# A hybrid diffusion layer on one core: the issue orders of five engine queues replaced in four stretches of the program

## The chip, the core and the metric

The kernel runs on one core of one Trainium2 chip. The metric is the device time of one execution in microseconds (us); the number that counts is the median over runs. The core's engines are named as in the profile: PE multiplies matrices (PEld loads its weights), DVE, ACT and POOL work on tiles in the on-chip memory, and SP does nothing here but issue DMA transfers. Each engine works off its own instruction queue strictly in order and waits at its head for what the next instruction needs.

## The reference, cut to what matters

One layer is applied to 512 latent and 128 context tokens (T = 640 together) of width D = 1024. The latent path in full (the context path is the same with one-dimensional convolutions):

```
mod = silu(cond) @ w_ada + b_ada                  # six vectors: sh1, sc1, g1, sh2, sc2, g2
h = rms_norm(x, g_mix_pre) * (1 + sc1) + sh1
z, xbc, dt_raw, cf_in = split(h @ w_in)
xbc = silu(dwconv1d(xbc, w_ssd_conv))
y = ssd(xbc, dt_f) + flip(ssd(flip(xbc), dt_b)) + xs * d_skip     # scans, forward and backward, 16 heads
y_ssd = rms_norm(y * silu(z), ssd_norm)
u = silu(layer_norm(dwconv1d(cf_a * sigmoid(cf_g), w_cf_conv)))   # 31 taps
x = x + g1 * rms_norm(concat(y_ssd, u) @ w_out, g_mix_post)
h = rms_norm(x, g_ffn_pre) * (1 + sc2) + sh2
f = (silu(gate) * val) @ w_down          # gate, val = halves of dwconv2d(h @ w_up), 3x3
x = x + g2 * rms_norm(f, g_ffn_post)
```

Outputs are both token sets and the two final scan states of the context.

## The kernel before, in words

**Layout.** Tokens lie along the free dimension, channels on the 128 partitions, so x is eight tiles `T_1` to `T_8` of 128x640 f32. Every large product is made in three matmuls of reduced precision: a weight tile `wr` of 128x1024 is split by ACT into a rounded part `wh` (line 320) and by POOL into the remainder `wl` (line 322), an activation into `H` (hi, ACT, line 409) and another `H` (lo, DVE, line 411), and `mm3` (line 424) adds w1·xh, w1·xl and w2·xh, each for 384 and 256 columns. Weight tiles come by SP into two buffers, `wh` and `wl` have three.

**Stages.** (1) First stage: SP loads the conditioning `cts`, the eight x tiles, 32 tiles of the adaLN weight (`in_wada`, 256 KB each, four groups of eight), the constants `csts` (the identity is in it), `prms`, `wdts` and the first projection weights (`wr_186`, `wr_192`, 512 KB each). ACT applies silu to `cts` (line 501), loads the table for the square root with a dummy instruction on `epsc` (line 503), and squares the x tiles into four rotating slots (line 507); PE sums the columns with a vector `ones` that POOL sets (lines 264 and 482); ACT takes the root (line 496), DVE the reciprocal (line 497), and PE spreads the result over the partitions with the identity (line 490). `ada_first(s)` multiplies one group of adaLN tiles with `cts` (line 450), ACT copies the sum to `adar` (line 453), PE transposes it (line 432) and DVE writes `modv` (line 441). DVE multiplies x by the spread reciprocal (line 532) and applies scale and shift (line 543); then hi, lo, the small product for dt (line 516) and the first three projections follow. (2) First quarter: the other projections, the two convolutions and eight pairs of scan heads. For each pair, rows of accumulated decays are loaded again from DRAM (`S<-acD`, lines 687 and 692), ACT subtracts them with a relu per chunk (line 798) and exponentiates (lines 782, 805); `ssd_states` copies states out of PSUM (line 757, tiles `S` or `AT`), POOL chains them, and PE uses them (lines 816, 827). (3) Middle norm: output projection, norm, `ada_half` for the second modulation (lines 465 to 472). (4) FFN up, convolution, down. (5) Tail: for each half of the columns `out_sums` (colsum, root, reciprocal), `out_spread` (line 1442; ACT copies the spread to `HL`, line 1446), `out_apply` (line 1449; multiply 1455, add 1456, store 1457), where POOL does pieces 0, 3 and 6 and DVE the other five.

**What sets the order.** The program text makes all instructions and their dependencies; the table `ORDER` (lines 49 to 172) then gives for each of the engines PE, DVE, Activation, Pool and SP a permutation of its instructions, as ranges of their numbers in program order. `issue_in_order` (line 175) ties each instruction to the one that the table puts ahead of it. So the table alone sets each queue, and the tiles, buffers and arithmetic come from the text. SP issues each DMA in that order as well, and a DMA waits for the one eight places ahead of it, whose semaphore it uses again.

Of the kernel before, what the change touches and what calls it, by code (L numbers as in the profile page):

```python
# [50 lines left out]
0-31 36-49 32-34 50-53 35 54-90 104-105 102-103 91-101 116-119 106 120-126 107-115 127 187-191 175-180 192  # L51
181-182 193 173-174 140-172 194-196 183-186 211-242 197-198 258-259 243 128-129 246-252 260-263 130-139
199-210 270 253-257 264-265 284-289 244-245 282-283 320-327 271-281 290-291 266-269 296 292-294 308-311
297-298 295 312-319 299-307 328-332 341-374 399-402 375-378 403 379-385 404 386-388 405-434 447-450 435-445
451-464 446 465-487 495 488-492 496-506 493-494 507-522 543-550 523 551-560 524-535 561-567 536 568-574
537-542 575-590 645-648 333-335 649-684 336-339 685-690 693-719 691-692 720-725 340 389-393 726-758 789-796
759 394-398 797-799 760-768 595 591-594 800-803 769-776 804-818 777-788 819-836 878-916 596-603 608 604-607
926-931 917-923 932-946 924-925 947-970 974-983 971-973 984-1005 609-620 1006-1014 1022 621-644 1023-1028
1015-1019 1029 1020-1021 1030-1048 837-841 1070-1073 1049 1074-1087 1050-1056 1088-1094 1057-1069 1095-1117
846-849 842-845 854-857 850-853 1118-1146 1207-1213 1147 1214-1216 1148-1163 1217 1164-1165 874-877 858-873  # L60
1218-1226 1255-1256 1227-1249 1257-1275 1250-1251 1276-1283 1252-1254 1284-1290 1170 1166-1169 1291-1294
1303-1314 1295-1302 1315-1337 1351-1352 1338-1350 1353-1374 1450-1452 1375-1381 1453-1470 1382-1398
1171-1178 1183-1186 1179-1182 1471-1484 1187-1206 1485-1517 1546 1518 1547-1554 1519-1521 1399-1403
1522-1524 1555-1556 1525 1557-1567 1526-1532 1568-1577 1533-1545 1578-1609 1683-1684 1610-1623 1404-1408
1624-1626 1685-1700 1627-1641 1701-1718 1409-1432 1441-1442 1433-1435 1443-1444 1436-1440 1719-1723
1731-1743 1724-1729 1744-1745 1730 1746-1755 1449 1445-1448 1756-1811 1827-1830 1812-1814 1642-1646
1815-1823 1831-1835 1824-1826 1836-1866 1916 1867 1917-1918 1647-1682 1919 1868-1869 1920 1870-1874
1921-2010 2012-2017 2011 2018-2022 1875-1879 2023-2080 2149-2150 2081-2089 2151-2157 2090-2103 2158-2164
2104-2107 2165-2179 1884-1887 1880-1883 1892-1895 1888-1891 2197-2201 1912-1915 1896-1911 2202-2244
2180-2196 2357-2386 2112 2108-2111 2245-2272 2387-2416 2117-2120 2113-2116 2417-2446 2125-2128 2121-2124  # L70
2145-2148 2129-2144 2447-2467 2507-2518 2468 2519 2273-2276 2317-2320 2277-2280 2321-2324 2469-2476
2520-2531 2477-2491 2325-2335 2341-2344 2336-2340 2281-2290 2492-2495 2291-2300 2496-2506 2532 2301-2310
2533-2534 2311-2312 2345-2352 2535-2545 2313-2316 2546-2552 2567-2585 2553-2562 2586-2593 2563-2566 2594
2353-2356 2597-2613 2595-2596 2614-2615 2810-2829 2759-2770 2645-2648 2621-2637 2649 2638-2639 2650-2658
2640-2641 2659-2661 2642-2644 2693-2704 2616-2620 2669-2676 2705-2709 2662-2668 2717 2710-2711 2677-2682
# [12 lines left out]
3397-3398 3374-3375 3380-3387 3399 3410-3412 3406-3409 3376-3377 3391 3378 3392-3393 3400-3402 3413-3414
# [1517 lines left out]
```

## Time and profile before

| | |
|---|---|
| runs | 976.6, 978.75 and 983.1 us, median 978.75 us |
| the profiled execution: own time, span | 980.17 us, 978.4 us |
| busy, share of the span | PE 945.8 us (97%), PEld 922.5 (94%), DVE 685.0 (70%), POOL 580.2 (59%), ACT 472.3 (48%) |
| the last chain, by engine | PE 89%, DMA 4%, ACT 2%, DVE 2% |
| DMA | 117.52 MB, mean 120 GB/s over the span |

The span runs from the first to the last instruction of the profiled execution; the execution's own time is 1.8 us longer. Idle time of PE is what is left to gain as long as the work stays the same, so the views used below list for an engine when it stood still and which instruction released it. In the lists of a timeline each row is a start, a duration, an engine, a line and an operation; in brackets stands the idle time just before and its releaser. The view of windows gives busy time per engine (with the number of instructions), the clock granted to PE, the share of time in which the DMA engines moved data, and the rate.

### The profile page before, as it was taken

The numbers are of one execution on the slowest core, as the hardware profiler recorded it, in microseconds if no ns is written. First come the engines' busy times: TensorE is split into PE (matmuls) and PEld (weight loads), VectorE is DVE, ScalarE is ACT, GpSimd is POOL, SyncE is SP. The second block draws the span as 40 slices with busy tenths as digits, with TensorE's granted clock in tenths as the row PEclk, the third lists the DMA queues.
The fourth block names the chain that finished last, engine by engine and source line by source line (L and its number), as shares of the span: only waits on it lengthen the run. The fifth ranks groups of instructions, "written<-read, shape, count | busy, mean of one in ns | idle before, by whom it ended". The sixth has DMA issues, their size and how long they took to land.

```text
span 978.4 us, 18784 instructions
## 1 busy us (share of the span) xinstructions
PE 945.8 (97%) x7623; PEld 922.5 (94%) x7623; DVE 685.0 (70%) x1076; ACT 472.3 (48%) x799; POOL 580.2 (59%) x416
## 2 busy tenths in 40 slices
PE   4999999999999999999999999999999999999995
PEld 2899999899999998999989999999999999999995
DVE  1769898888989997633576897998988898400004
ACT  4345665877568495822454843323233336322211
POOL 1334699798999882634761997444454436543434
PEclk9999999999999999999999999999999999999998
DMA  9622424434325342589661243222222231322213
GB/s 344 254 71 83 121 82 127 117 100 146 118 84 161 87 125 76 160 274 325 204 213 56 68 168 97 80 83 69 87 65 86 66 87 55 96 67 76 82 38 108
DMA packets 50294, 117.52 MB, mean 120 GB/s; under 512 B 6016, under 2 KB 13952, under 8 KB 50208
## 3 DMA queue, kind: packets, MB, share of 16 engines
q1 hardware_dynamic: 50208, 116.33, 37.4%
q8 instruction: 60, 0.98, 0.4%
q14 instruction: 26, 0.21, 0.1%
HBM read 112.55 MB, written 3.75 MB: 119 GB/s over the span
## 4 chain that ended last, share of the span: by engine, by line
PE 89%; DMA 4%; ACT 2%; DVE 2%; issue 1%; POOL 1%; SPq 1%; POOLq 0%; ACTq 0%
PE ps L424 75%; PE ps L1268 2%; PE pq L424 2%; PE pq L827 2%; PE pq L469 2%; PE pq L816 1%; DMA T<-in_wada 1%; DMA S<-acD 1%; PE pq L753 1%; PE pq L450 1%; DMA S<-in_wada 1%; DMA wr<-in_wup 1%; PE pq L1268 1%; PE pq L601 1%; PE pq L490 1%
## 5 line engine op out<-in xcount | busy, mean ns | idle before, releaser
L322 POOL TENSOR_TENSOR wl<-wr,wh 128x1024 fp32r<-128x1024 f32 (+3 forms) x127 | 290.5, 2291 | 320.3 <-ACT wh L320 297.7
L424 PE MATMUL ps<-H,wh 128*128 128x384 f32 (+1 forms) x1636 | 316.9, 309 | 0.1
L424 PE MATMUL ps<-T,wh 128*128 128x384 f32 (+1 forms) x1472 | 272.7, 306 | 0.3 <-ACT S L1236 0.3
L320 ACT ACTIVATE wh<-wr 128x1024 fp32r<-128x1024 f32 (+3 forms) x131 | 131.3, 1003 | 288.8 <-PE ps L424 179.9
L1246 DVE SCALAR_TENSOR_TENSOR S<-ps,prms,S 128x441 f32<-128x441 f32 (+2 forms) x336 | 233.4, 695 | 28.9 <-ACT S L1236 18.3
L424 PEld LDWEIGHTS ps<-H,wh 128*128 128x128 f32 x1636 | 249.8, 188 | 2.9 <-issue 1.7
L424 PEld LDWEIGHTS ps<-T,wh 128*128 128x128 f32 x1472 | 218.9, 188 | 0.8 <-ACT S L1236 0.6
L881 DVE SCALAR_TENSOR_TENSOR ps<-u,prms,ps 128x655 f32<-128x655 f32 x205 | 185.1, 903 | 12.0 <-ACT ps L878 6.1
L424 PE MATMUL ps<-H,wl 128*128 128x384 f32 (+1 forms) x818 | 191.6, 309 | 0.0
L424 PE MATMUL ps<-T,wl 128*128 128x384 f32 (+1 forms) x736 | 166.2, 305 | 0.0
L424 PEld LDWEIGHTS ps<-H,wl 128*128 128x128 f32 x818 | 129.1, 188 | 1.0 <-issue 1.0
L497 DVE RECIPROCAL rsm<-rsm 128x160 f32<-128x160 f32 (+2 forms) x9 | 7.4, 817 | 152.0 <-ACT rsm L496 152.0
L424 PEld LDWEIGHTS ps<-T,wl 128*128 128x128 f32 x736 | 113.0, 188 | 0.0
L424 PE MATMUL ps<-S,wh 128*128 128x384 f32 (+1 forms) x420 | 88.1, 310 | 0.0
L424 PEld LDWEIGHTS ps<-S,wh 128*128 128x128 f32 x420 | 66.4, 188 | 1.2 <-issue 0.6
L424 PE MATMUL ps<-S,wl 128*128 128x384 f32 (+1 forms) x210 | 54.8, 310 | 0.0
L798 ACT ACTIVATE S<-S,AC 128x128 f32<-128x128 f32 x140 | 45.5, 392 | 3.6 <-DMA S<-acD 3.6
L894 POOL TENSOR_TENSOR T<-T,T 128x640 f32<-128x640 f32 x20 | 32.0, 1600 | 13.8 <-ACT T L890 13.8
L1236 ACT ACTIVATE S<-ps,prms 128x640 f32<-128x640 f32 x42 | 36.6, 871 | 4.1 <-PE ps L1268 3.7
L424 PEld LDWEIGHTS ps<-S,wl 128*128 128x128 f32 x210 | 35.1, 188 | 0.5 <-POOL wl L322 0.2
L890 ACT ACTIVATE T<-u,prms 128x512 f32<-128x512 f32 (+1 forms) x54 | 27.9, 554 | 6.8 <-POOL T L894 6.8
L1348 POOL TENSOR_TENSOR H<-S,S 128x640 f32<-128x640 f32 x16 | 25.3, 1582 | 3.3 <-DVE S L1249 3.2
(346 smaller groups left out, 1189.1 us busy)
## 6 DMA issues: line engine op xcount, KB each, us to landing
wr<-in_wup SPq DMA_DIRECT2D x44, 512.0 KB, 3.5
wr<-in_win SPq DMA_DIRECT2D x36, 512.0 KB, 3.9
T<-in_wada SPq DMA_DIRECT2D x49, 256.0 KB, 5.4
S<-acD SPq DMA_DIRECT2D x28, 320.0 KB, 4.7
wr<-in_wdown SPq DMA_DIRECT2D x16, 512.0 KB, 3.5
wr<-in_wout SPq DMA_DIRECT2D x13, 512.0 KB, 4.2
H<-in_wada SPq DMA_DIRECT2D x23, 256.0 KB, 5.0
S<-in_wada SPq DMA_DIRECT2D x16, 256.0 KB, 5.4
```

The costliest lines, as they stand in the source:

```text
L320: ac.activation(hi[:, :n], raw[:, :n], AF.Copy)
L322: lo_eng.tensor_tensor(lo[:, :n], raw[:, :n], hi[:, :n].bitcast(F32), SUB)
L424: last_mm[0] = te.matmul(out, w, x[:, c0:c1], start=first and i == 0, stop=last and i == 2)
L469: te.matmul(pt[32 * j:32 * j + 32, 0:P], cts[:, kc, :], w[:, j * P:(j + 1) * P], start=kc == 0, stop=kc == KD - 1, tile_position=(0, 32 * j))
L798: ac.activation(rc, rc, AF.Relu, scale=-1.0, bias=AC2[:, c, row:row + 1])
L881: ve.scalar_tensor_tensor(acc, u[:, j:j + UO], w(j), acc, MUL, ADD)
L890: ac.activation(t[:, b:c], u[:, a:a + c - b], AF.Copy, scale=w(j))
L894: gp.tensor_tensor(far, far, t, ADD)
L1236: ac.activation(out, v, AF.Identity, bias=prm_col("ffn_b", i), scale=w(1, 1))
L1246: ve.scalar_tensor_tensor(ob, vl[:, r0 + a - 1:r1 + a - 1, q0 + b - 1:q1 + b - 1], w(a, b), ob, MUL, ADD)
L1268: te.matmul(pt[:, o:o + c1 - c0], w[k] if i in (1, 2) else w[:, k * P:(k + 1) * P], x[:, c0:c1], start=k == 0 and j == 0, stop=k == KD - 1 ...
L1348: gp.tensor_tensor(f_raw[q], a, b, MUL)
```

## The change

Nothing but the table `ORDER` changes; it has nine more lines, so every line number below it is nine higher in the changed kernel. All tiles, matmuls, transfers and dependencies are the same. Activation-table loads, which the compiler inserts where the function changes, are 16 instead of 14. The diff's core (the first lines of two of its five lists):

```diff
 ORDER = {
     "PE": """
-0-31 36-49 32-34 50-53 35 54-90 104-105 102-103 91-101 116-119 106 120-126 107-115 127 187-191 175-180 192
...
+0-27 36 28-31 37-67 32 68 33-35 69-87 102 88-91 103 92-100 104 116 101 105-106 117-118 107 119 108 120-125
...
     "SP": """
-0-8 14 24 10 13 16 11 9 12 15 23 19 17 31 27 25 18 20 26 28-29 41 47 30 36 34-35 38 40 21 43 39 37 44-45 42
...
+16 4 11 0 19 1 6 18 5 2-3 12 7-8 10 14 13 15 20 17 9 24 29 27 26 25 28 23 30-31 36 41 35 39 37 34 38 33 21
```

On SP the new order begins with an adaLN tile, x4, an adaLN tile, `cts` and `wr_186` (5th; it was 20th), then x1, x6, `prms` (8th; it was 25th), x5, x2, x3, an adaLN tile, x7 and x8 (14th; it was 9th); `wr_192` is 19th (26th), the last tile of adaLN group 0 20th (21st), `csts` 21st (16th); the last tile of group 1 is 30th (32nd). DVE scales tile `T_1` alone first, and PE does all of `ada_first(0)` ahead of the spread, where the two were mixed.

The head of ACT's queue. Tiles `S_18` to `S_25` are the squares, `T_1` to `T_8` the x tiles. Before:

```order
L501 ACT_TABLE_LOAD
L501 ACTIVATE cts<-cts 128x256
L503 ACT_TABLE_LOAD
L503 ACTIVATE warm<-epsc 128x1
L507 ACTIVATE S_18_128<-T_1_71 128x640
L507 ACTIVATE S_19_134<-T_2_73 128x640
```

and in the changed kernel:

```order
L329 ACT_TABLE_LOAD
L329 ACTIVATE wh_188<-wr_186 128x1024
L516 ACTIVATE S_21_146<-T_4_77 128x640
L516 ACTIVATE S_18_128<-T_1_71 128x640
L510 ACT_TABLE_LOAD
L510 ACTIVATE cts<-cts 128x256
L516 ACTIVATE S_19_134<-T_2_73 128x640
L516 ACTIVATE S_20_140<-T_3_75 128x640
L516 ACTIVATE S_22_152<-T_5_79 128x640
L516 ACTIVATE S_23_158<-T_6_81 128x640
L516 ACTIVATE S_24_164<-T_7_83 128x640
L516 ACTIVATE S_25_170<-T_8_85 128x640
```

The split of the first weight tile now stands ahead of all squares, and the dummy root has left the head: the root's table is loaded after the last square. On POOL's queue, in the same place, the changed kernel has

```order
L331 TENSOR_TENSOR wl_190<-wr_186,wh_188 128x1024
L273 MEMSET ones 128x1
L275 MEMSET epsc 128x1
L279 MEMSET u_111 128x15
L331 TENSOR_TENSOR wl_196<-wr_192,wh_194 128x1024
```

where `ones` was POOL's first instruction of the kernel's own and `wl_190` came after all memsets: now the vector that the column sums use is set behind the first weight remainder.

ACT's queue between the first and the second pair of scan heads. `S_168` to `S_171` are the rows of decays, `T_181` belongs to the 31-tap convolution, `wh_2004` is a weight split, and `S_186` a transposed tile. Before:

```order
L320 ACTIVATE wh_1901<-wr_1899 128x1024
L320 ACTIVATE wh_2004<-wr_2002 128x1024
L603 ACTIVATE S_186_1668<-pq_187_1669 128x512
L603 ACTIVATE S_186_1668<-pq_188_1675 128x128
L890 ACTIVATE T_181_1577<-u_119,prms 128x512
L890 ACTIVATE T_181_1577<-u_119,prms 128x128
L798 ACTIVATE S_169_1410<-S_169_1410,AC_715 128x128
L798 ACTIVATE S_170_1412<-S_170_1412,AC_715 128x128
```

and in the changed kernel:

```order
L807 ACTIVATE S_169_1410<-S_169_1410,AC_715 128x128 x2
L329 ACTIVATE wh_2004<-wr_2002 128x1024
L899 ACTIVATE T_181_1577<-u_119,prms 128x512
L612 ACTIVATE S_186_1668<-pq_187_1669 128x512
L612 ACTIVATE S_186_1668<-pq_188_1675 128x128
L899 ACTIVATE T_181_1577<-u_119,prms 128x128
L807 ACTIVATE S_169_1410<-S_169_1410,AC_715 128x128
L807 ACTIVATE S_168_1408<-S_168_1408,AC_715 128x128
```

Two relus of row tile `S_169` moved ahead of the weight split, the convolution pieces and the transposed tile. On SP the four row loads of this pair now go out in the order `S_170`, a weight tile, `S_169`, `S_168`, and later `S_171`; the weight tile stood ahead of all four.

DVE's queue in the tail, where `rsm_10635` is the reciprocal for the second half of the columns and the tiles of 128x384 belong to the first half. Before:

```order
L1455 TENSOR_TENSOR S_851_10117<-S_851_10117,pq_863_10524 128x384
L1456 TENSOR_TENSOR S_851_10117<-S_851_10117,M_565_5313 128x384
L1455 TENSOR_TENSOR S_854_10274<-S_854_10274,pq_863_10524 128x384
L1456 TENSOR_TENSOR S_854_10274<-S_854_10274,M_578_5418 128x384
L1455 TENSOR_TENSOR U_860_10510<-U_860_10510,pq_863_10524 128x384
L497 RECIPROCAL rsm_10635<-rsm_10635 128x64
L1456 TENSOR_TENSOR U_860_10510<-U_860_10510,M_586_5557 128x384
```

and in the changed kernel:

```order
L1464 TENSOR_TENSOR S_851_10117<-S_851_10117,pq_863_10524 128x384
L1464 TENSOR_TENSOR S_854_10274<-S_854_10274,pq_863_10524 128x384
L1465 TENSOR_TENSOR S_845_9803<-S_845_9803,M_539_5109 128x384
L1465 TENSOR_TENSOR S_854_10274<-S_854_10274,M_578_5418 128x384
L506 RECIPROCAL rsm_10635<-rsm_10635 128x64
L1464 TENSOR_TENSOR U_860_10510<-U_860_10510,pq_863_10524 128x384
L1465 TENSOR_TENSOR S_851_10117<-S_851_10117,M_565_5313 128x384
```

The reciprocal now comes after seven of the ten first-half operations, where it came after nine. The tail's stores on SP and POOL's pieces are permuted too. Elsewhere (the rest of the first quarter, the middle norm) the orders of ACT, POOL, DVE and SP are permuted by a few places throughout, PE's in single groups of at most a few matmuls; from the FFN up-projection to the tail they are almost unchanged.

More of the change, by code (lines that the diff above doesn't have):

```diff
@@ L56 @@
[L56 to L75, printed above, removed]
@@ new lines @@
+1568-1577 1533-1545 1578-1609 1683-1684 1610-1623 1404-1408 1624-1626 1685-1700 1627-1641 1701-1718
+1409-1432 1441-1442 1433-1435 1443-1444 1436-1440 1719-1723 1731-1743 1724-1729 1744-1745 1730 1746-1755
+1449 1445-1448 1756-1811 1827-1830 1812-1814 1642-1646 1815-1823 1831-1835 1824-1826 1836-1866 1916 1867
+1917-1918 1647-1682 1919 1868-1869 1920 1870-1874 1921-2010 2012-2017 2011 2018-2022 1875-1879 2023-2080
+2149-2150 2081-2089 2151-2157 2090-2103 2158-2164 2104-2107 2165-2179 1884-1887 1880-1883 1892-1895
@@ new lines @@
+1888-1891 2197-2201 1912-1915 1896-1911 2202-2244 2180-2196 2357-2386 2112 2108-2111 2245-2272 2387-2416
+2117-2120 2113-2116 2417-2446 2125-2128 2121-2124 2145-2148 2129-2144 2447-2467 2507-2518 2468 2519
+2273-2276 2317-2320 2277-2280 2321-2324 2469-2476 2520-2531 2477-2491 2325-2335 2341-2344 2336-2340
+2281-2290 2492-2495 2291-2300 2496-2506 2532 2301-2310 2533-2534 2311-2312 2345-2352 2535-2545 2313-2316
+2546-2552 2567-2585 2553-2562 2586-2593 2563-2566 2594 2353-2356 2597-2613 2595-2596 2614-2615 2810-2829
@@ new lines @@
+5549-5596 5616-5658 5693-5695 5659-5664 5696-5716 5665-5692 5717-6386 6389 6387 6390 6388 6391-6519 6521
+6520 6522-6583 6587 6584 6588 6585-6586 6589-6591 6596-6597 6665 6598-6599 6666-6668 6600-6603 6592-6595
+6604-6664 6669-6676""",
+    "DVE": """
+0-3 13-16 4 19 18 17 5 20 11-12 23-24 26 25 6 27-29 7-8 30 9-10 21 33-34 22 36 35 39 37 31 41 32 42 38 43 47
+46 44 40 45 48 51-52 49-50 53-54 84-85 55 86-88 56 89 111-112 69 113 90 114 91-96 119-120 57 121-122 58 97
+59-61 98 62-64 99-100 65 101-102 66-67 123 68 70 75 103-104 124 105 125 71 106 72 107 73 108 76 152 77
@@ new lines @@
+1060 1066 1068 1064 1070-1072 1069 1073 1067 1074-1075""",
+    "Activation": """
+11 5 2 0 3-4 6-10 12 15 18-19 17 21-22 13 20 24 23 25 27 26 32-33 14 28-30 16 35 47 56 48 31 57 61 58 49 1
+64 62 34 51 67 65 63 50 66 52 79 37 53 38 54 39-40 80 41 116 36 55 45 42 120 43 68 44 46 59 117 71 69-70
+121-122 60 96 72 90 73-74 86 81 88 97 123 101 75-76 87 103 82 78 99 77 83 133 94 100 89 110 95 98 112 91 134
+92 166 108 102 104 84-85 124 127 170 125 128 126 107 106 167 105 129 93 109 171 111 130 173 172 113-115 135
@@ new lines @@
+693 691 695 692 694 698 696 700 697 699 703 701 727 705 702 704 708 706 709 707 714 710-713 715 719 716
+725-726 717 720 731 718 723 721-722 732 724 728-729 733-734 730 735 741 736-740 745 742-744 746-747 751
+748-750 752-753 757 754-756 758-760 763-765 769 761 770 766-767 771 762 768 772 775-778 773 779-780 783-784
+774 781-782""",
+    "Pool": """
+11 0-2 12-13 19 3 16-18 4 14-15 24 10 7 25 9 26 20 27 5 21 33 6 22 65 23 69 28-30 70 35 31 75 36 8 34 93 50
+37-38 32 39 51 40-41 71 42-44 49 45 48 97 46-47 52-56 98 57 72 64 66 58-61 67 77 73 62 74 63 76 103 80 104
@@ L172 @@
+284-286 278 276 287-289 281-282 279 277 283 280 290-343 346 349-350 347 344 351 345 356 348 354-355 357
+352-353 359 358""",
 }
```

190 lines of the change are left out of this document (95 added, 95 removed).

## The prediction

> **What bounds the kernel now.** I read the busy shares first, then the windows, the list of waits, and last the timelines of single engines at the places where PE stood still.
>
> ```profile
> PE 945.8 (97%) x7623; PEld 922.5 (94%) x7623; DVE 685.0 (70%) x1076; ACT 472.3 (48%) x799; POOL 580.2 (59%) x416
> ```
> ```profile
> 0.00:10.00 10.00, 1.38 (x16) 0.43 (x16) 0.00 (x0) 4.83 (x7) 0.72 (x15) 1.00 0.79 270
> 10.00:20.00 10.00, 6.34 (x91) 4.39 (x91) 1.15 (x1) 5.23 (x8) 0.12 (x1) 1.00 1.05 395
> 20.00:30.00 10.00, 7.81 (x109) 4.44 (x106) 7.89 (x16) 2.87 (x5) 4.60 (x2) 0.83 1.06 393
> 170.00:180.00 10.00, 8.01 (x52) 7.84 (x51) 8.69 (x15) 9.97 (x22) 7.04 (x4) 0.83 0.42 122
> 560.00:950.00 390.00, 390.00 (x2762) 389.60 (x2761) 251.72 (x399) 131.51 (x170) 205.49 (x105) 1.00 0.27 82
> ```
> ```profile
> PE pq L482 <- ACT S L507: 11.9, 3, 5.5
> PE pq L816 <- ACT AT L757: 2.0, 1, 2.0
> PE ps L1268 <- ACT wh L320: 1.4, 1, 1.4
> PE pq L469 <- ACT AT L1039: 1.0, 1, 1.0
> ```
>
> PE does the same matmuls before and after, so only its idle time can move: 978.4 - 945.8 = 32.6 us. The windows say where it is: 8.6 us in the first ten, 3.7 in the next, 2.2 in the third, 2.0 between 170 and 180, and none in the 390 us from 560 to 950. After PE's end at 970.3 another 8.1 us belong to the tail. The waits put 11.9 of the first stage on the squares. A reordering that leaves PE full from 560 to 950 cannot win more than a few us in each of four small places, and it can lose in any of them. The granted clock of 0.83 in two windows of 10 us is, if it was 0.5 for a while and 1.0 otherwise, 0.17 x 10 / 0.5 = 3.4 us at half speed, 1.7 us lost where PE is full.
>
> **First stage, the start of the chain.** The rows that price it:
>
> ```profile
> 2.82 0.42 ACT L501 ACTIVATE cts<-cts 128x256 f32<-128x256 f32 x1 [0.82 <-DMA cts<-in_ct]
> 3.25 1.28 ACT L503 ACT_TABLE_LOAD   x1
> 9.69 1.99 ACT L507 ACTIVATE S<-T 128x640 f32<-128x640 f32 x3 [3.61 <-DMA T<-in_xT]
> 16.98 0.39 ACT L496 ACTIVATE rsm<-pq,epsc 128x160 f32<-128x160 f32 x1 [1.35 <-PE pq L482]
> 18.74 1.06 ACT L320 ACTIVATE wh<-wr 128x1024 fp32r<-128x1024 f32 x1 [1.36 <-DMA wr<-in_win]
> ```
> ```profile
> 25.47 2.36 POOL L322 TENSOR_TENSOR wl<-wr,wh 128x1024 fp32r<-128x1024 f32 x1 [3.22 <-ACT wh L320]
> ```
> ```profile
> 17.41 1.15 DVE L497 RECIPROCAL rsm<-rsm 128x160 f32<-128x160 f32 x1 [17.41 <-ACT rsm L496]
> 20.56 1.55 DVE L532 TENSOR_TENSOR T<-T,ps 128x640 f32<-128x640 f32 x2 [2.00 <-PE ps L490]
> ```
>
> Behind `wr_186`, now fifth on SP, everything queues on ACT and POOL: all squares, silu, `wl_190`, and `ones` with every column sum behind it. Through it 1.51 MB have to land (262 + 328 + 262 + 131 + 524 KB). Before, 0.13 MB were there at 2.8 us and 2.10 MB (with the sixth x tile) at 9.7, so 1.51 MB take until 7.6 by a straight line; the first pieces came slower, so I take 8.1. `wh` ends at 9.2, `wl` at 11.5, `ones` at 11.7. On ACT after 9.2: two squares (1.4), table (1.28), silu (0.42), six squares at 0.73 (4.4): 16.7. The root's table can't lie in idle time any more as it did at 3.25; it runs from 16.7 to 18.0, beside the last column sum, then root 0.39, reciprocal 1.15: 19.6, against 17.41 + 1.15 = 18.56. The spread needs `csts`, now 21st, with 6.1 MB through it: 2.7 MB in ten us, the rest at 394 GB/s, about 1 us to settle: 19.7. From the reciprocal to DVE's first x product it took 2.0 us (18.56 to 20.56) with adaLN matmuls between; I take 1.8 without most of them. So DVE starts at about 21.5, 1.0 later.
>
> **First stage, the end of the chain.** PE is what counts, and it waited for something else:
>
> ```profile
> 24.18 2.00 PE L450 MATMUL pq<-S,cts 128*32 128x128 f32 x28 [0.94 <-DMA S<-in_wada]
> 26.11 0.90 PE L424 MATMUL ps<-H,wh 128*128 128x384 f32 x2
> 27.80 1.08 PE L450 MATMUL pq<-S,cts 128*32 128x128 f32 x13
> 29.36 0.33 PE L432 MATMUL pq<-csts,adar 128*128 128x128 f32 x1 [0.47 <-ACT adar L453]
> ```
> ```profile
> 24.48 0.82 DVE L411 TENSOR_TENSOR H<-T,H 128x640 fp32r<-128x640 f32 x1
> 26.05 2.46 DVE L411 TENSOR_TENSOR H<-T,H 128x640 fp32r<-128x640 f32 x1
> ```
>
> The products are continuous from 29.4 on, when adaLN group 1 is through; its last tile was the 32nd transfer and is the 30th now, two tiles of 262 KB fewer, 0.52 MB at 393 GB/s = 1.3 us. Before, its last 13 matmuls ran until 28.9, mixed with others at half clock; 1.3 us earlier and at full clock they end at about 26.5. The first H lo ends at about 25.9 (25.3 before) and feeds it; the second took 2.46 us instead of 0.82, in the same stretch as POOL's `wl` (25.47 to 27.83), which is done earlier now. So PE is full from 26.5, 2.9 us earlier; 0.9 us of products that it had done before 29.4 are still to do. **Term: -2.0 us.** Bounds: if all eight transfers in flight share the rate, `wr_186` lands with 2.2 MB at about 10.2, the whole head shifts by 2.1, H lo to 28.0, and PE idles 1.5 us of it; with a cold clock besides (1.5, below) +1.0. If the 0.44 us wait for the third modulation goes too, and the saving is the full 2.9: -3.4.
>
> The Trainium skill ("ScalarE: Activation LUTs", What ACT_TABLE_LOAD costs) puts a switch of table at about 2.66 us, of which 1.38 are a drain behind the load of 1283 ns; it speaks against the two more table loads here. The trace shows 1283 ns and the next activation within 0.02 us (958.42 + 1.28, next 959.71, below). By the page the root would come 1.4 us later and the term be -0.6.
>
> **First quarter.** The place is the first pair's states.
>
> ```profile
> 156.84 1.06 ACT L320 ACTIVATE wh<-wr 128x1024 fp32r<-128x1024 f32 x1 [4.60 <-PE ps L424]
> 160.00 0.77 ACT L603 ACTIVATE S<-pq 128x512 f32<-128x512 f32 x2 [2.10 <-PE pq L601]
> 160.65 1.02 ACT L890 ACTIVATE T<-u,prms 128x512 f32<-128x512 f32 x2
> 164.01 0.70 ACT L798 ACTIVATE S<-S,AC 128x128 f32<-128x128 f32 x2 [2.34 <-DMA S<-acD]
> 165.20 2.75 ACT L798 ACTIVATE S<-S,AC 128x128 f32<-128x128 f32 x9 [0.49 <-DMA S<-acD]
> 173.40 0.58 ACT L757 ACTIVATE AT<-pq 128x512 f32<-128x512 f32 x1
> ```
>
> ACT used its wait for the rows of decays: 2.85 us of other work (1.06 + 0.77 + 1.02) lay ahead of the relu that waited until 164. Now two relus stand ahead of that work, so it comes after the landing. `S_169` should land earlier, at about 162.9, since one row load of 328 KB fewer is ahead of it. From there ACT needs what it needed before (173.98 - 164.01 = 10.0), plus 2.85, less the 0.49 wait inside and about half a us of convolution pieces that went behind the copy: 11.8, or 174.7, and PE waits 0.7 us longer. **Term: +0.7 us**, bounded by -3.7 (the whole wait of 2.0 goes, and with it the half clock in that window, 1.7) and by +3.0 (the row lands no earlier, and ACT's later copies slip too). The rest of the quarter is a finer mixing at unchanged waits, hidden by a PE that is full; cost nothing, unless the first rival holds.
>
> **Middle norm.** The waits of 1.4 (behind a weight split) and 1.0 us can each go or grow; nothing in the order is tied to either, since the PE rows around them stay and their releasers move by a few places. **Term: 0**, from -2.4 (both gone) to +1.5 (the longer one doubled).
>
> **Tail.**
>
> ```profile
> 958.42 1.28 ACT L496 ACT_TABLE_LOAD   x1
> 959.71 0.34 ACT L496 ACTIVATE rsm<-pq,epsc 128x96 f32<-128x96 f32 x1
> 967.70 0.31 ACT L496 ACTIVATE rsm<-pq,epsc 128x64 f32<-128x64 f32 x1
> ```
> ```profile
> 968.03 0.54 DVE L1455 TENSOR_TENSOR U<-U,pq 128x384 f32<-128x384 f32 x1
> 968.50 0.54 DVE L497 RECIPROCAL rsm<-rsm 128x64 f32<-128x64 f32 x1
> ```
> ```profile
> 969.04 1.25 POOL L1456 TENSOR_TENSOR U<-U,M 128x384 f32<-128x384 f32 x1
> 970.75 0.73 POOL L1455 TENSOR_TENSOR H<-H,HL 128x256 f32<-128x256 f32 x1 [0.46 <-ACT HL L1446]
> ```
>
> The second root is ready at 968.01, and DVE, which was busy until 968.5, has two operations fewer (some 1.3 us) ahead of the reciprocal and takes it at once: 0.47 earlier. Spread, copy and POOL's last six pieces follow it; but POOL is only free at 970.29, so it gains its idle 0.46 and no more. **Term: -0.45 us**, from -0.7 to +0.3 (a store behind a later one in the new SP order).
>
> **The sum**: -2.0 + 0.7 + 0 - 0.45 = -1.75 us against the profiled execution's span of 978.4: 976.65, and 978.4 as its own time (980.17). That execution lies 1.4 us above the median of the runs, 978.75; against the median it is **977.0 us**.
>
> **The rivals.**
> (1) *Slower: head-of-line blocking by the row loads.* What happens at the first pair may happen at all eight, since relus that wait for rows now stand between copies that PE waits for throughout. For it: ACT is 9.97 of 10 us busy at 170 to 180. Against it: in the list of waits only one pair shows a wait of this size. Each further pair costs a wait like the 2.0 + 0.7 and a half clock behind it (1.7): 4.4 us; it decides from three pairs on: 977.0 + 13.2 = 990 us.
> (2) *Faster: the waits close together.* The 2.0 with its half clock, the 1.4 and 1.0 of the middle, the whole -3.4 of the first stage and the -0.7 of the tail: -3.7 - 2.4 - 3.4 - 0.7 = -10.2, 968.5 us. For it: each of these waits ends on ACT, which is busy less than half of the span. Against it: the first pair's new order lengthens the largest of them.
> (3) *The gain does not arrive: DVE sets the pace of the first stage.* DVE is 7.89 of 10 us busy from 20 to 30 and starts its x products 1.0 us later. If PE follows it, the first term is +1.0 and the sum +1.25: 980 us. Against it: these 7.89 us hold the remainder of 2.46 us that takes 0.82 elsewhere, 1.6 us to spare.
> (4) *PE starts cold.* Matmuls of one kind took 421 ns at 16.7 and 276 ns at 20.4:
>
> ```profile
> L450 PE MATMUL pq<-T,cts 128*32 128x128 f32 x16 | 1.1, 421 | 0.0
> L450 PE MATMUL pq<-T,cts 128*32 128x128 f32 x28 | 1.1, 276 | 0.0
> ```
> ```profile
> 14.00:17.68 3.67, 3.65 (x60) 2.90 (x64) 0.26 (x1) 1.13 (x2) 0.00 (x0) 1.00 1.06 393
> ```
>
> Between the two lies this window, 3.7 us in which PE was busy throughout. Now the column sums come one square at a time until 17.2, with gaps, and the change may come one stretch of 3.4 us later: group 0 and the spread then take 1 to 2 us longer, and the first term shrinks to -0.5: 978.5 us. The Trainium skill ("TensorE: Matmul & The Clock Gate", What's actually happening) states this as a rule: half rate by default, full after a busy window of about 3.4 us, windows that run freely; the trace agrees, with 421 and 276 ns.
>
> **How the numbers follow.** Chances: forecast 0.46, gain lost (3) 0.22, cold start (4) 0.10, slower (1) 0.12, faster (2) 0.10. The forecast's own range is 973 to 981, its terms' bounds not all at one end. The range for 8 in 10 goes from 969.5 to 985: it takes in the cases (3) and (4), most of the way to (2) and the high ends of the terms (+1.0 + 3.0 + 1.5 + 0.3 = +5.8, 984.6), and leaves out (1). About 1% is what a measurement of this kernel can tell from no change. Only (2) reaches beyond it on the fast side (968.9), by little: 0.10; on the slow side (above 988.5) case (1): 0.12; within it 0.78.
>
> **What would show it.** Right: PE's column sums start near 11.7 instead of 5.5 us, DVE's x products near 21.5, PE is full from about 26.5; the wait for `AT` near 175 is 2 to 3.5 us; POOL's last six pieces start 0.4 us after its first-half pieces would allow, that is without idle time. Wrong: products that are not continuous before 29, waits for `ACT` copies in several pairs, new waits of over 2 us in the middle norm, or a granted clock of 0.5 in more than two places.

## The result, and the profile after

| | before | after |
|---|---|---|
| median of 13 runs each, on one chip | 978.45 us (975.97 to 983.1) | 984.16 us (981.43 to 986.22) |
| ratio | 1 | 1.0061, 95% interval 1.0049 to 1.0073 |
| the profiled execution: own time, span | 980.17, 978.4 us | 982.7, 980.9 us |

The changed kernel is slower by 5.7 us, 0.6%. That time lies inside the range given and within 1% of the kernel before, but the forecast pointed the other way, to 1.75 us less.

The two profiled executions differ by only 2.5 us, since that of before holds two stretches of 3.4 us at a granted clock of 0.5 (24.5 to 27.9 and 174.7 to 178.1 us), and that of after has none between 16 and 971.7 us. Such stretches come and go from run to run, so below the trace of the first experiment (the kernel before with the changed first stage alone, 974.6 us, no such stretch either) often stands in for the kernel before.

The first line of busy shares, the windows that answer to those of before, with three more from the first quarter, and PE's longest waits, all of the changed kernel:

```profile
PE 944.7 (96%) x7623; PEld 920.2 (94%) x7623; DVE 685.6 (70%) x1076; ACT 473.9 (48%) x801; POOL 579.2 (59%) x416
```
```profile
0.00:10.00 10.00, 0.00 (x0) 0.00 (x0) 0.00 (x0) 2.22 (x2) 0.20 (x4) 1.00 0.79 272
10.00:20.00 10.00, 5.90 (x120) 3.75 (x120) 0.78 (x1) 8.98 (x14) 2.46 (x4) 1.00 1.04 393
20.00:30.00 10.00, 7.64 (x103) 5.81 (x104) 7.94 (x21) 2.99 (x6) 2.35 (x1) 1.00 1.04 361
120.00:130.00 10.00, 9.23 (x65) 9.01 (x64) 9.68 (x13) 9.24 (x21) 9.20 (x6) 1.00 0.20 68
170.00:180.00 10.00, 8.15 (x62) 7.77 (x61) 9.67 (x16) 10.00 (x22) 9.81 (x9) 1.00 0.22 65
220.00:230.00 10.00, 8.65 (x87) 8.03 (x86) 9.89 (x15) 4.61 (x8) 9.39 (x10) 1.00 0.04 14
244.00:254.00 10.00, 9.21 (x63) 8.69 (x62) 9.75 (x13) 8.98 (x17) 10.00 (x6) 1.00 0.35 99
```
```profile
PE pq L491 <- POOL u L279: 12.6, 1, 12.6
PE pq L459 <- DMA S<-in_wada: 2.0, 1, 2.0
PE pq L825 <- ACT AT L766: 1.7, 1, 1.7
PE pq L459 <- DMA T<-in_wada: 1.3, 1, 1.3
PE pq L499 <- DVE rsm L506: 1.0, 1, 1.0
PE ps L433 <- ACT u L870: 1.0, 2, 0.5
PE ps L433 <- POOL wl L331: 0.9, 2, 0.5
PE ps L433 <- ACT S L807: 0.8, 1, 0.8
```

PE's busy time is about that of before, the wait of 2.0 us at the first pair has become 1.7, and the longest new waits lie in the first 25 us. What is new after that is a row of waits of 0.3 to 0.8 us (on ACT, POOL and DVE in turn) that before did not have. In the kernel with the changed first stage alone, three of the same windows are full; there PE stands still in 170 to 180 only:

```profile
120.00:130.00 10.00, 10.00 (x72) 10.00 (x72) 9.36 (x13) 7.34 (x15) 9.08 (x6) 1.00 0.38 118
170.00:180.00 10.00, 8.61 (x66) 8.45 (x65) 9.67 (x16) 9.97 (x21) 7.00 (x5) 1.00 0.41 133
220.00:230.00 10.00, 10.00 (x93) 9.63 (x92) 9.12 (x15) 6.20 (x13) 9.41 (x9) 1.00 0.44 116
244.00:254.00 10.00, 10.00 (x74) 10.00 (x74) 9.61 (x12) 6.32 (x14) 9.77 (x9) 1.00 0.40 118
```

Waits alone do not add up to 5.7 us. So I also compared starts of the same matmul, at places where both kernels have issued the same set of matmuls (minus: the second kernel is earlier):

| place, us | before to after | first stage alone to after |
|---|---|---|
| 30 | -1.6 | +1.0 |
| 41 | -1.1 | +1.0 |
| 53 | -0.3 | +1.1 |
| 71 | 0.0 | +1.1 |
| 126 | +0.9 | +2.1 |
| 172 | +1.3 | +2.4 |
| 180 | -0.7 (before has its half clock just ahead) | +2.9 |
| 207 | -0.1 | +3.6 |
| 226 | +0.8 | +4.5 |
| 252 | +1.9 | +5.6 |
| 345 | +2.6 | +6.4 |
| 534 | +1.8 | +5.7 |
| 970 | +1.5 | +5.2 |

The right column grows by 4.5 us between 71 and 252 us and has changed by less than one us more at any later place of the table: the loss has a place. (The first row's 1.0 us lies in the first transfers, where both kernels have the same order; executions of that head differ by up to 2 us there.) The middle column says that the first stage's lead of 1.6 us is gone by 71 us, in windows in which PE counts as busy for 10.00 of 10 us. The half clock at 24.5 us of this trace of before is not the reason: in each of the six traces with the old head, one without that stretch among them, the old head makes up 1.5 to 1.6 us on the changed kernel between 30 and 71 us. Records of successive matmuls overlap, here by 0.16 us, so a wait shorter than the overlap would show in no list:

```profile
123.78 0.45 PE L433 MATMUL ps<-H,wl 128*128 128x384 f32 x2
124.07 0.73 PE L433 MATMUL ps<-H,wh 128*128 128x384 f32 x4
```

On ACT, the relu on the rows of decays is the group whose idle time grew most (before it had 3.6 us), and on SP the row loads wait longer. The changed kernel, the page's group and SP's own waits; behind them the same two lines of the first-stage kernel:

```profile
L807 ACT ACTIVATE S<-S,AC 128x128 f32<-128x128 f32 x140 | 46.6, 393 | 20.8 <-DMA S<-acD 20.8
```
```profile
SPq L696 <- PE pq L836: 79.2, 6, 21.0
```
```profile
L798 ACT ACTIVATE S<-S,AC 128x128 f32<-128x128 f32 x140 | 45.6, 392 | 3.9 <-DMA S<-acD 3.9
```
```profile
SPq L687 <- PE pq L827: 49.6, 6, 15.4
```

### The profile page after: what moved, and what is told of

It reads as the page before. It is cut to its first block, busy times and chain, and to the rows that moved or that the text cites. A ratio compares the mean times of both kernels' runs of the same rounds, so it can differ in the third digit from the quotient of the medians.

```text
span 980.9 us, 18803 instructions
## 1 busy us (share of the span) xinstructions
PE 944.7 (96%) x7623; PEld 920.2 (94%) x7623; DVE 685.6 (70%) x1076; ACT 473.9 (48%) x801; POOL 579.2 (59%) x416
## 4 chain that ended last, share of the span: by engine, by line
PE 81%; POOL 5%; DMA 5%; DVE 3%; ACT 3%; issue 2%; SPq 1%; POOLq 0%; ACTq 0%; DVEq 0%
PE ps L433 68%; PE ps L1277 3%; PE pq L433 2%; DMA S<-acD 2%; PE pq L478 1%; POOL wl L331 1%; PE pq L836 1%; DVE ps L890 1%; PE pq L825 1%; DMA T<-in_wada 1%; ACT S L807 1%; DMA T<-in_xT 1%; PE pq L459 1%; DMA S<-in_wada 1%; POOL S L818 1%
## 5 line engine op out<-in xcount | busy, mean ns | idle before, releaser
L807 ACT ACTIVATE S<-S,AC 128x128 f32<-128x128 f32 x140 | 46.6, 393 | 20.8 <-DMA S<-acD 20.8
L433 PEld LDWEIGHTS ps<-S,wl 128*128 128x128 f32 x210 | 35.2, 188 | 0.9 <-POOL wl L331 0.8
```

The lines of the kernel that those rows point to most:

```text
L433: last_mm[0] = te.matmul(out, w, x[:, c0:c1], start=first and i == 0, stop=last and i == 2)
L807: ac.activation(rc, rc, AF.Relu, scale=-1.0, bias=AC2[:, c, row:row + 1])
```

## The experiments

Two families of theories were open: the loss sits in one stretch, or in one list; and within a stretch, in one engine's pace, one late copy, or one transfer.

**Which stretch.** Five kernels take the five lists of one kernel for some of the time and those of the other for the rest. The cuts lie where both orders have issued the same instructions on an engine (80, 390 and 560 us), but for one place: on POOL, the kernels with a cut at 80 us and the new order behind it on that engine (quarter, and below act, sp and half2) have one weight remainder ahead of a product of the 31-tap convolution that the changed kernel issues first.

```diff
 # kernel        to 80   80-390  390-560  from 560
-before          old     old     old      old
+first           new     old     old      old
+quarter         old     new     old      old
+middle          old     old     new      old
+tail            old     old     old      new
+noquarter       new     old     new      new
```

> The table of before, with the changed order only in the first stage (up to about 80 us; every list of the table is cut there, and the later rest is that of before). Theory A (the loss arises among the scan pairs, the first stage breaks even because its earlier products are given back before 70 us): within 1 us of before, that is 977.5 to 979.5. Rival B (the late column sums are what costs): slower by 3 to 5 us, 981 to 984. Rival C (parts only lose together): within 1 us as well, as the next three would be too.

> The table of before, with the changed order only from about 80 to 390 us (projections, convolutions, scan pairs). Theory A: slower by 3.5 to 5 us, 982 to 983.5, with PE waits of 0.3 to 0.8 us near 125, 206, 225, 245 and 252 us as in the changed kernel. Rival B: within 1 us. Rival C: within 1 us.

> The table of before, with the changed order only from about 390 to 560 us (output projection, middle norm, start of the up-projection). Theory A: faster by 0.5 to 1 us, since the lead of before over the changed kernel falls from 2.7 to 1.7 us in this stretch. Rivals B and C: within 0.5 us.

> The table of before, with the changed order only from about 560 us to the end, where it differs in the tail alone. Theory A: slower by 0.5 to 1 us, since DVE and not POOL ends last there (DVE's adds beside POOL took 0.7 to 0.9 us instead of 0.5). The prediction had 0.45 us faster here. Rival C: within 0.3 us.

> The changed kernel with the order of before from about 80 to 390 us (all five engines). If the loss sits in that stretch (theory A), this lies within 1.5 us of before, 977 to 979. If the parts lose only together (rival C), it stays 3 us or more above before.

| kernel | median, us | ratio to before, 95% |
|---|---|---|
| first | 978.73 | 1.0005 (0.9990 to 1.0019) |
| quarter | 987.98 | 1.0098 (1.0078 to 1.0119) |
| middle | 977.84 | 0.9995 (0.9978 to 1.0013) |
| tail | 978.73 | 1.0007 (0.9993 to 1.0022) |
| noquarter | 978.27 | 1.0008 (0.9996 to 1.0021) |

The whole loss comes from 80 to 390 us: without that stretch nothing measurable is left of the change, and alone it costs more than in the changed kernel (9.6 against 6.0 us by the ratios). In the trace of the quarter alone PE waits 1.98 us for DVE at 93 us, which it does not do in the changed kernel, and a half clock of 3.4 us follows; between 71 and 100 us this trace loses 3.9 us on the changed kernel, about what the stretch alone costs on top (9.6 less 6.0). The likely reading is that the new quarter fits the new head; it was not tried apart. The first stage, for which 2.0 us had been forecast, measures +0.5 (-1.0 to +1.9).

**Which list.** The changed kernel with one engine's list of before between 80 and 390 us.

```diff
 # 80-390 us     ACT  SP   POOL  PE, DVE
-after           new  new  new   new
+act             old  new  new   new
+sp              new  old  new   new
+pool            new  new  old   new
```

> The changed kernel with ACT's list of before from about 80 to 390 us, the other four lists as changed. Theory A1 (on ACT, relus that wait for the rows of decays now stand ahead of the copies out of PSUM and the weight splits that PE waits for): 3.5 to 5 us faster than the changed kernel, 979 to 980.5, and the waits of PE near 125, 206 and 245 us gone. Rival A2 (SP brings the rows later, whatever ACT's order): 1 to 2 us faster at most. Rival A3 (POOL's and DVE's lists: weight remainders and evacuations late): no change, 983 to 985.

> The changed kernel with SP's list of before from about 80 to 390 us, the other four lists as changed. Theory A1: 0 to 2 us faster than the changed kernel, since the relus still stand ahead of the copies and only their wait gets shorter. Rival A2: 3.5 to 5 us faster, 979 to 980.5, with ACT's idle time ahead of the relus back from 20.8 us to about 4. Rival A3: no change.

> The changed kernel with POOL's list of before from about 80 to 390 us, the other four lists as changed. Theory A1 and rival A2: within 1 us of the changed kernel, 983 to 985. Rival A3: 2 to 4 us faster, 980 to 982.

Measured: 992.3 us, 1.0138 (1.0118 to 1.0158); 987.07, 1.0103 (1.0085 to 1.0120); 995.93, 1.0195 (1.0175 to 1.0214). Each swap makes it worse, by 4 to 13 us. In act and sp about 1 us of it goes with the place on POOL named above: PE waits 1.0 and 0.7 us for DVE near 95 us there. So these runs blame no list; the lists of one stretch seem to fit each other, and an old list among new ones is a misfit of its own. One thing could be read from the run with SP's old list: there the fourth pair of heads takes 35.2 us, as before, and not 36.7.

**Which half.** The changed kernel with before's order from 80 to 187 us (half1) or from 187 to 260 us (half2).

```diff
 # changed kernel, all five lists
+half1:  80-187 us old, the rest new
+half2: 187-260 us old, the rest new
```

> The changed kernel with the order of before from about 80 to 187 us (all five engines). From the traces the changed order loses 1.8 us against before in that stretch (at 125 and 171 to 175 us): theory A gives 982 to 983, the rival that all is lost in one place gives 984 (none here) or 979 (all here).

> The changed kernel with the order of before from about 187 to 260 us (all five engines). From the traces the changed order loses 3 us there, in pieces of 0.3 to 0.7 at 206, 226, 245 and 251 us: theory A gives 980.5 to 981.5; the rival that all is lost in one place gives 984 or 979.

Measured: 981.17 us, 1.0038 (1.0023 to 1.0052), and 982.33 us, 1.0052 (1.0032 to 1.0072). Against 1.0061 the first half gives back 2.2 us, the second 0.9. Both halves carry a part of it, the two together 3 of the 6 us by the times. The traces say more. Against the first-stage kernel, the changed one loses 1.8 us between 80 and 190 us and half1 0.2; from 190 to 300 us the changed one loses 3.2 and half2 0.4. So each half holds its own loss, and half2 has a new one of 1.0 us between 71 and 100 us, from the place on POOL (PE waits 0.7 us for DVE at 93.6 us), which hides about as much of its gain.

**Late copies, and other single suspects.** In the changed kernel some groups of matmuls are copied out of PSUM late, 2.6 us after their last matmul where the first-stage kernel has 0.3, since ACT and DVE have other pieces ahead. evac moves four such copies forward; ps251 moves eight matmuls back behind the second pair's products; rows issues the row loads of pairs 2 to 4 together and earlier; ones_first sets the vector of ones ahead of the first weight remainder, so that the wait of 12.6 us at the head no longer hangs on it.

```diff
 # table ORDER of the changed kernel
 evac, "Activation"
-227 208 200 229 199 198 228 ... 270 261 271 279 280
+227 228 208 200 229 199 198 ... 279 280 270 261 271
 evac, "DVE"
-140 141 164 165 142 ... 265 266 249 250
+164 165 140 141 142 ... 249 250 265 266
 ps251, "PE"
-1218-1225 874-877 858-873 1226
+874-877 858-873 1218-1226
 rows, "SP" (one of the places)
-107 105 86 111 128 108 106 112
+107 105 108 106 86 111 128 112
 ones_first, "Pool"
-11 0 1 2
+0 11 1 2
```

> The changed kernel with four copies out of PSUM moved forward in their queues, nothing else: the second part of a copy on ACT directly behind its first (near 204 us, ahead of two relus, a weight split and two more relus), a pair on ACT ahead of two exponentials and a relu (near 243), a pair on DVE ahead of two taps of the 31-tap convolution (near 123) and a pair of products with PSUM ahead of two taps (near 224). Theory D (what the changed order loses are copies out of PSUM that stand behind other work, so that a later group of matmuls waits for the bank): PE's waits of 0.77, 0.51, 0.66 and 0.47 us at 125, 206, 226 and 245 us go or halve, 1 to 2.4 us faster than the changed kernel, 981.5 to 983. Rival E (the rows of decays and weight remainders are late, the copies only stand at the end of the same chain): the waits reappear within 10 us elsewhere, and the time stays at 983.5 to 984.5.

> The changed kernel with eight matmuls of a projection put back behind the last products of the second pair of heads on PE (near 187 us), where before had them. Theory R (the chain from one pair's products over the loads of decay rows, ACT's relus and exponentials to the next pair's products sets the time here): the second pair's products end 1.2 us earlier, and so does everything behind: 982 to 983.3. Rival P (PE is full there and only its waits count): no change, 983.5 to 985.

> The changed kernel with the four loads of full decay rows of pairs two, three and four issued one behind the other on SP, ahead of the half rows, stores and weight tiles that stand between them. Theory R with SP as the late link: pair periods 33.6, 39.3 and 36.7 us shrink by 0.5 to 2 us each, 981 to 983. Theory R with ACT or DVE as the late link, and rival P: no change, 983.5 to 985.

> The changed kernel with the vector of ones set first on POOL again, ahead of the first weight remainder. The largest wait in the list, 12.6 us of PE for POOL's memsets, goes: the column sums start at about 10 us, behind the first squares. Theory A and D: the time stays within 0.5 us of the changed kernel, since the last square and the last adaLN tiles set when the stage ends. Rival B (late column sums and a cold clock cost the first stage): 1 to 2 us faster.

Measured: evac 984.72 us, 1.0073 (1.0054 to 1.0092); ps251 984.48, 1.0069 (1.0047 to 1.0090); rows 988.23, 1.0092 (1.0072 to 1.0111); ones_first 984.66, 1.0083 (1.0062 to 1.0105). None helps. With evac PE's gap at 125 us is gone, as meant, and its waits on other engines are longer instead:

```profile
PE ps L431 <- POOL wl L329: 2.4, 3, 1.0
PE pq L760 <- POOL S L746: 2.0, 2, 1.1
```

These two (the first with a gap at 251.4, the second at 129.9 and 171.7 us) were 0.9 and 0.2 us in the changed kernel. So a late copy is not the cause of the gap behind it; it stands in the way of something that is late anyway. rows made the fourth pair longer (40.2 us; why is told below). In ones_first PE waits 11.6 us for ACT's squares instead, and the time is no better: the place of the vector, named by the most striking wait of the new list, costs nothing. The late-copy theory fell with evac.

**DVE's pace.** Both kernels with every second multiply-add of the 31-tap convolution cut to 128 of 655 columns, so part of the convolution is left out; each such tap takes DVE 0.35 us instead of 0.90.

```diff
-            ve.scalar_tensor_tensor(acc, u[:, j:j + UO], w(j), acc, MUL, ADD)
+            m = UO if j % 2 else 128
+            ve.scalar_tensor_tensor(acc[:, 0:m], u[:, j:j + m], w(j), acc[:, 0:m], MUL, ADD)
```

> The kernel before with every second tap of the 31-tap convolution on DVE over 128 instead of 655 columns; part of the convolution is left out, so about 65 us of DVE's 185 in these taps go. If DVE's queue sets the pace in the pairs: 5 to 15 us faster than before. If PE does: within 3 us, only its waits of 2.0 and 0.7 us shrink.

> The changed kernel with the same cut of the convolution's taps on DVE. If what the changed order loses is work on DVE that stands ahead of PE's releases: the difference to before falls from 5.7 us to under 2. If it is lost in row loads and ACT's queue, with DVE only filling the time: the difference to the kernel before with the same cut stays at 4 to 6 us.

Measured: 977.67 us, 0.9996 (0.9982 to 1.0009) from before, and 982.27 us, 1.0044 (1.0028 to 1.0059) from after. The kernel before does not get faster by less work on DVE; the changed one gets some 1.7 us back (the intervals of 1.0044 and 1.0061 overlap), and 4.6 us of difference stay. The trace says where: against the first-stage kernel, the steps of 1.0 and 0.7 us at 126 and 226 us are gone, and 0.6 appears at 132 us. Around 125 us the list of waits names ACT, but the chain that ended last runs through DVE from 118 us on, and at 226 us PE waits for DVE by the list too. So at these two places the changed order is held up by DVE's queue; at the others the cut takes nothing away.

**One link.** The fourth pair of scan heads (from the third pair's y products on PE to the fourth's) takes 36.7 us after and 35.2 before. In the trace the difference begins at ACT, which waits for a weight tile, the load of which SP issued behind four transfers (two row loads, a store and a load of half rows), the first of which waits for pair 3's products. The changed kernel, ACT first, then SP, then PE's matmul that uses the remainder of a tile split later:

```profile
235.81 1.06 ACT L329 ACTIVATE wh<-wr 128x1024 fp32r<-128x1024 f32 x1 [3.13 <-DMA wr<-in_win]
```
```profile
228.48 1.31 SPq L696 DMA_DIRECT2D S<-acD  x2
229.84 0.42 SPq L767 DMA_DIRECT2D out_nsb<-AT  x1
230.37 0.45 SPq L701 DMA_DIRECT2D S<-acD  x1
230.92 0.53 SPq L305 DMA_DIRECT2D wr<-in_win  x1
```
```profile
252.01 0.56 PE L433 MATMUL ps<-H,wl 128*128 128x384 f32 x2 [0.32 <-POOL wl L331]
```

The last two kernels move that one number of SP's list, 128, in both directions:

```diff
 # load_ahead: changed kernel, "SP"
-115 119 107 105 86 111 128 108
+115 119 128 107 105 86 111 108
 # load_behind: kernel before, "SP"
-115 119 128 86 105 107 111-112 108
+115 119 86 105 107 111 128 112 108
```

> The changed kernel with one row of SP's list moved: the load of the weight tile wr_2829 stands ahead of pair 4's row loads again (as in the kernel before), not behind four of them. Theory L (weight load behind the row loads): the load starts near 217 us instead of 231, ACT's conversion of it no longer waits (3.1 us at 236 in the changed kernel), the fourth pair takes 35.2 to 35.9 us instead of 36.7, the PE gap near 252 goes, and the time is 982.5 to 983.5 (1 to 1.5 us less than the changed kernel's 984.2). Rival (the loss is spread over many small waits and this link only shows it): the conversion is early, but the pair still takes 36.4 us or more and the time stays 984.0 to 984.7.

> The kernel before with the same row of SP's list moved the other way: the load of wr_2829 stands behind three row loads and one half row of pair 4, as in the changed kernel. Theory L: ACT waits about 2 to 3 us ahead of that tile's conversion, the fourth pair takes 36.4 to 37.0 us instead of 35.2, and the time is 979.6 to 980.2 (978.4 before). Rival: the load has enough lead in this order, the pair stays at 35.2 to 35.5 us and the time at 978.0 to 978.8.

On their chip the kernel before took 977.25 us; load_ahead took 982.77, 1.0052 (1.0032 to 1.0072), load_behind 979.24, 1.0012 (0.9994 to 1.0030). By the time alone the effect is too small to be told from none. The traces tell it. Of load_ahead: the load on SP, the split on ACT, the third and the fourth pair's y products on PE:

```profile
223.85 0.33 SPq L302 DMA_DIRECT2D wr<-in_win  x1
```
```profile
232.24 1.05 ACT L326 ACTIVATE wh<-wr 128x1024 fp32r<-128x1024 f32 x1
```
```profile
225.88 2.40 PE L833 MATMUL pq<-S,S 128*64 128x128 f32 x40 [0.63 <-DVE S L824]
```
```profile
261.06 2.46 PE L833 MATMUL pq<-S,T 128*64 128x128 f32 x40
```

and of load_behind the split, the third pair's products, the same late remainder as in the changed kernel, and the fourth pair's products:

```profile
233.22 1.06 ACT L318 ACTIVATE wh<-wr 128x1024 fp32r<-128x1024 f32 x1 [4.07 <-DMA wr<-in_win]
```
```profile
223.01 2.40 PE L825 MATMUL pq<-S,S 128*64 128x128 f32 x40
```
```profile
249.60 0.56 PE L422 MATMUL ps<-H,wl 128*128 128x384 f32 x2 [0.36 <-POOL wl L320]
```
```profile
260.22 2.49 PE L825 MATMUL pq<-S,T 128*64 128x128 f32 x40
```

The pair takes 261.06 - 225.88 = 35.2 us with the load ahead and 260.22 - 223.01 = 37.2 with it behind (36.7 in the changed kernel, 35.2 in the first-stage kernel, 256.94 - 221.77). Moved one way, the number takes the wait on ACT, PE's gaps near 245 and 252 and 1.5 us of the pair out of the changed kernel; moved the other way, it puts all three into the kernel before. The kernel rows is one more point: there the same load stands behind six transfers, and ACT waits longer still:

```profile
241.67 1.06 ACT L326 ACTIVATE wh<-wr 128x1024 fp32r<-128x1024 f32 x1 [5.70 <-DMA wr<-in_win]
```

Its pair takes 40.2 us, of which an estimated 1.7 (half of 3.4) are lost to a half clock in it. Counted from the third pair's products, the split begins after 6.4 us in load_ahead, 9.6 in the changed kernel, 10.2 in load_behind and 12.2 in rows, and the pairs take 35.2, 36.7, 37.2 and 40.2. The link is shown, with one trace of each kernel: a load of a weight tile, queued on SP behind row loads that wait for PE, costs the pair that needs the tile 1.5 to 2.0 us. load_ahead does not keep all of it: its third pair is slower, 39.9 us against 39.3.

## Why the prediction was wrong

**The failed step** is one sentence of the first-quarter term: "The rest of the quarter is a finer mixing at unchanged waits, hidden by a PE that is full; cost nothing, unless the first rival holds." I priced one place of a stretch of 310 us in which four lists were permuted throughout, and the stretch costs the loss: 1.0061 less 1.0008, 5.2 us, where the term said +0.7. By pairs, in us from one pair's y products to the next, in the first-stage kernel and the changed one: 31.8 and 33.6, 38.9 and 39.3, 35.2 and 36.7, 30.0 and 30.0, 40.6 and 40.7, 31.0 and 31.3; ahead of the first pair another 1.2 us. Of the 1.8 of the second pair, 1.2 are no loss: the new PE list puts the eight matmuls of ps251 ahead of its products.

By starts of the same matmul, the 5.2 us that the changed kernel's trace loses on the first-stage kernel's from 80 to 380 us fall into six pieces. 1.0 at 126 us and 0.7 at 226 hang on DVE's queue, by the trace with half of the taps cut. 1.6 between 240 and 256 us are the link on SP: load_ahead loses 0.1 there. 0.8 between 172 and 176 us are the place that I priced; SP issues the last of that pair's four row loads 5.3 us later, at 160.39, where PE is only some 2 us later, but no run moved that load alone. For 0.8 at 206 to 210 us, where PE waits for a copy on ACT, and 0.3 behind 260 us the cause stays open: evac moved that copy forward, and PE lost 1.4 us there. So the step put two queues at nothing that were not: SP's, with a weight tile behind row loads, and DVE's.

**The place that I did price came out as worked out.** The changed kernel, ACT around the first pair:

```profile
162.99 0.70 ACT L807 ACTIVATE S<-S,AC 128x128 f32<-128x128 f32 x2 [11.87 <-DMA S<-acD]
174.53 0.59 ACT L766 ACTIVATE AT<-pq 128x512 f32<-128x512 f32 x1
```
```profile
175.17 0.94 PE L825 MATMUL pq<-M,S 128*128 128x128 f32 x6 [1.67 <-ACT AT L766]
```

The row landed at 162.99 (forecast 162.9), the copy began at 174.53 (174.7). PE's wait was 1.67 instead of 2 to 3.5, since PE itself came later. The 11.87 us of idle time ahead of the relus is most of the 20.8 of the whole group, and PE passes the place with 0.4 us more than the first-stage kernel (2.4 and 2.9 in the table), 0.8 with the 0.4 just ahead of it, where 0.7 had been forecast.

**First rival.** Head-of-line blocking by the row loads was right in kind: it is what the shown link is, with a weight tile behind the loads rather than copies behind the relus. The price of 4.4 us for a pair was too high; no pair loses more than 1.6 us. I had tied the rival to new entries like that of 2.0 us in the list of waits. The loss came in waits of 0.3 to 0.8 us.

**First stage, -2.0: near at 30 us, worth little at 71.** The changed kernel's head, ACT, then DVE, then PE:

```profile
9.07 1.06 ACT L329 ACTIVATE wh<-wr 128x1024 fp32r<-128x1024 f32 x1 [7.05 <-DMA wr<-in_win]
17.50 1.28 ACT L505 ACT_TABLE_LOAD   x1 [0.64 <-PE pq L491]
18.80 0.39 ACT L505 ACTIVATE rsm<-pq,epsc 128x160 f32<-128x160 f32 x1
```
```profile
19.22 1.16 DVE L506 RECIPROCAL rsm<-rsm 128x160 f32<-128x160 f32 x1 [19.22 <-ACT rsm L505]
22.30 0.82 DVE L541 TENSOR_TENSOR T<-T,ps 128x640 f32<-128x640 f32 x1 [0.59 <-PE ps L499]
```
```profile
12.64 0.76 PE L491 MATMUL pq<-S,ones 128*32 128x160 f32 x8 [12.64 <-POOL u L279]
24.58 1.07 PE L459 MATMUL pq<-S,cts 128*32 128x128 f32 x30 [1.96 <-DMA S<-in_wada]
```

`wh` begins 1.0 us later than worked out (9.07 against 8.1), the column sums 0.9 (12.64 against 11.7; 11.63 in the trace of the first-stage kernel with the same head), the reciprocal ends at 20.4 instead of 19.6 and DVE's x products begin at 22.3 instead of 21.5; PE is continuous from 24.6, earlier than the 26.5 of the forecast. The matmuls behind it are 1.6 us ahead of before at 30 us. What failed is the assumption that a lead on PE lasts, and with it "PE does the same matmuls before and after, so only its idle time can move": between 30 and 71 us the same 386 matmuls take 1.58 us more in the new mix, and no two of them start more than 0.43 us apart (0.71 before), so no single wait does it. first and noquarter put the term at +0.5 and, with the small middle and tail, +0.8 us. That is the third rival's result (the gain does not arrive), but not shown to be its cause: what sets the pace of the projections, be it the mix itself, DVE's second half tiles or the weights, was not tried.

By the Trainium skill ("ScalarE: Activation LUTs", What ACT_TABLE_LOAD costs) the root would have come 1.4 us later than the load's end. The trace does not show that drain, and the measurement decides: 17.50 + 1.28 = 18.78, and the root starts at 18.80.

**Cold start.** The granted clock of 1.00 in the first windows proves nothing, since the kernel before shows it too where its matmuls took 421 ns. The matmuls themselves tell it: in the changed kernel the column sums take 475 ns each until 15 us and the adaLN products 273 ns from 16.5 us on, where before had 421 ns until 17.5. The full rate comes earlier, not one stretch later; the fourth rival fell.

**Middle, 0:** 0.9995 (0.9978 to 1.0013), as forecast.

**Tail, -0.45: the reciprocal as forecast, the end not.** The second root ends at 969.98 and the reciprocal starts at 970.01, where before it waited 0.49 us. But now DVE ends last, not POOL. The changed kernel, DVE and POOL:

```profile
972.18 0.42 DVE L1464 TENSOR_TENSOR H<-H,pq 128x256 f32<-128x256 f32 x1
974.52 1.47 DVE L1465 TENSOR_TENSOR S<-S,M 128x256 f32<-128x256 f32 x2
975.91 0.94 DVE L1465 TENSOR_TENSOR H<-H,M 128x256 f32<-128x256 f32 x1
977.22 0.50 DVE L1465 TENSOR_TENSOR U<-U,M 128x256 f32<-128x256 f32 x1
```
```profile
972.22 0.73 POOL L1464 TENSOR_TENSOR S<-S,HL 128x256 f32<-128x256 f32 x1 [0.54 <-ACT HL L1455]
975.67 0.90 POOL L1464 TENSOR_TENSOR U<-U,HL 128x256 f32<-128x256 f32 x1
976.65 0.79 POOL L1465 TENSOR_TENSOR U<-U,M 128x256 f32<-128x256 f32 x1
```

From the first piece of the second half to the last one's end it takes 977.72 - 972.18 = 5.54 us, before 975.81 - 970.71 = 5.10; from there to the end of the span 3.2 us, before 2.6. The 0.47 won at the reciprocal is given back twice over by about 0.4 and 0.6. The run of the tail alone (+0.7, -0.7 to +2.2) can't tell +0.5 from 0. I had counted POOL's idle time (0.46 before, still 0.54 after: the sign that I named as right did not show) and left out what its pieces do to DVE's: the addition of 975.91 takes 0.94 us and ends 0.28 us behind the POOL operation in which it began (976.85 and 976.57; more below).

## What to carry to other kernels

A permutation of whole lists can't be priced at its most visible wait: walk along the bottleneck engine and compare the start of the same instruction at many places, since losses of 0.3 to 0.8 us, and a new mix of the same matmuls, add up unseen in a window that reads "full". On an in-order DMA queue, ask of every load what waits ahead of it: a weight tile with two buffers put behind transfers that wait for PE stalls its split, then everything behind the split, and at last PE. And a lead at the head of a program counts only if nothing later sets the pace; here 1.6 us were gone within some 40 us. When orders are joined in time, check on every engine that both have issued the same instructions at the seam: one misplaced weight remainder on POOL cost 1.0 us here.

## What the runs showed of the hardware

- An operation on DVE that reads two tiles in the on-chip memory waits for one that POOL has under way. In the changed kernel, 42 such operations of 128x640 began while POOL had no tensor operation running, and all took 0.81 to 0.83 us; of 26 that began within one, 22 ended 0.68 us behind POOL's end, whatever their length (1.81 us at 220.13). The nine of 128x256 that began within one ended 0.28 us behind it. Before shows the same 0.68 (22 of 25) and 0.28 (10 of 11). This was read from the traces, not isolated by a run.
- The stretches of 3.4 us at half clock fall behind a pause of PE of 1 to 3 us (24 and 172 to 176 us, 251 us in rows), in some executions and not in others of nearly the same order: with before's order at 174.7 us, in the first-stage kernel with a similar wait not at all. In a single profile such a stretch is worth 1.7 us (half of 3.4, an estimate), a third of the effect that was looked for.
